# Gate and up projections with 512 moving columns behind one stationary operand

## The chip, the cores and the metric

The kernel runs on one core of a Trainium2 chip. The metric is device time in microseconds (us). The engines are named as the profile does: PE is TensorE (matmuls), PEld its weight loads, DVE is VectorE, ACT is ScalarE, POOL is GpSimd, and SP is the queue from which the DMAs are issued. A matmul has a stationary operand (lhsT, loaded first) and a moving operand, whose columns stream past it; the result is added up in a PSUM bank, which holds 512 fp32 columns for 128 partitions.

## The reference

Two layers of a trunk. Each makes modulation vectors, one input projection for two groups of heads (a gated delta rule and an attention), an output projection, a layer norm, and a SwiGLU feed-forward part with a second layer norm. 128 context tokens and 128 latent tokens go through the same weights, each group with its own modulation. The part that is changed is the feed-forward part:

```python
D_MODEL = 2048
D_FF = ((8 * D_MODEL + 767) // 768) * 256      # 5632
...
    h = x * (1.0 + sc2) + sh2
    gate, up = jnp.split(h @ w_gate_up, 2, axis=-1)
    ffn = (jax.nn.silu(gate) * up) @ w_down
    x = layer_norm(DN_ALPHA * x + g2 * ffn, ln2_g, ln2_b)
```

All is fp32.

## The kernel before

**Numbers in two halves.** The matmuls run in the type fp32r. To come near fp32, each operand is split: H is the value rounded to fp32r, L the rest. A product is then three passes: activation H by weight H, activation L by weight H, activation H by weight L. `wtile` brings two pairs of weight blocks with one DMA of 1 MB (tile `r`) and splits each pair: ACT copies to H (L391), DVE subtracts to L (L392). H and L have three buffers each, the DMA tiles four, which they share with the modulation weights (`rt`, `ra`).

**Gate and up.** The 5632 columns of gate and of up are cut into 22 chunks of 256 + 256 columns. A chunk runs over the 2048 rows of the weight, 16 blocks of 128, in four tiles `g` of four blocks. `col_mm` does one tile: for each half j of the tile (two blocks) and each of four groups b of 128 output columns (two of gate, two of up) the weight is stationary, and the 256 tokens are the moving columns. Lines L422 (H by H), L423 (activation L by weight H) and L426 (activation H by weight L) issue four, by blocks, and two matmuls. Two groups share a bank: `acc[0]` holds gate, `acc[1]` up. They come from the pool psA, which has three banks.

At the end of a chunk ACT takes the tanh of gate (L1234, tile `fth`), DVE makes silu (L1235) and the product with up (L1237, `hx`), and ACT (L1240) and DVE (L1241) split that into H and L of the hidden activations (`dH`, `dL`).

**Down.** After 16, 16 and 12 blocks of hidden columns the down projection runs over what is there (`HALVES`), in four column blocks of 512, with the hidden activations stationary and 512 weight columns moving (`row_mm`, L399, L400, L402). The result is added to `y`.

**Beside it.** In the feed-forward part of layer 0 DVE also computes modulation vectors of the next layer as dot products (`ada_dot`, L242, tile `rt`; a step is one DMA tile and two instructions, 16 steps a vector; four vectors in layer 0, one in layer 1). `fill` issues steps at a rate: `RATES[l][2]` is 0.55 in layer 0 and 0.15 in layer 1, and a quarter of it is added at each call, of which a chunk has 16. The order of instructions on each engine is set by the scheduler of the framework at build time; each engine then works in that order.

**Before and after.** The activations `h2` of the gate and up matmuls are built from the normed `y` by transposes into PSUM (L475), a modulation (L480 on DVE, L482 on ACT) and the split (L485, L486). The transposes use banks of the pool psG, whose tag `gu` has three. The same SBUF places hold, in turn, `h`, `mix` and `h2`, in four tiles hH0, hL0, hH1, hL1 of eight blocks each. The last column block of the down projection is kept for the `tail`, which runs the two token groups one after the other, so that the norm of one runs beside the matmuls of the other.

Of the kernel before, what the change touches and what calls it, by code (L numbers as in the profile page):

```python
# [106 lines left out]
def trunk(ctx: ExitStack, tc: tile.TileContext, A: dict, O: dict):  # L107
# [303 lines left out]
    def col_mm(acc, W, act, kts, first, last, hook=None):  # L411
        for j, (H, L) in enumerate(W):
# [3 lines left out]
            for b in range(4):  # L416
# [10 lines left out]
                if hook is not None and b % 2 == 1:  # L427
                    hook()

    def acc2():  # L430
        return [psA.tile([128, 512], F32, tag="acc", name="acc") for _ in range(2)]

    class Act:


        def __init__(self, tiles, per):
            self.t, self.per = tiles, per

# [4 lines left out]
        def stat(self, part, kt, s):  # L443
            return self.span(part, kt, 1)[:, 0, s, :]

        def mov(self, part, kt):
            return self.span(part, kt, 1)[:, 0].rearrange("p s t -> p (s t)")

    def new_act(name):
        return Act([tuple(htp.tile([128, 8, 2, 128], F32R, tag=f"h{x}{i}", name=f"{name}{x}{i}") for x in "HL")  # L450
                    for i in range(2)], 8)

# [157 lines left out]
    def mixer(l, h_act, P, first_layer, ax, xsrc, prev):  # L610

        W = A["p_in"][l]
        if True:
# [253 lines left out]
            def scratch(name, wide=False):  # L867

                if not first_layer:
                    return slab(name)[:, 0:1024 if wide else 512]  # L870
                if not scr:
                    scr["n"] = htp.tile([128, 2048], F32, tag="hH0", name="scr0")
                    scr["w"] = htp.tile([128, 2048], F32, tag="hL0", name="scr1")
# [323 lines left out]
    for l in range(NL):  # L1197
# [7 lines left out]
        with ExitStack() as fx:  # L1205
# [17 lines left out]
            for part, nkt in enumerate(HALVES):  # L1223
                hid = Act([(hidp.tile([128, 16, 2, 128], F32R, tag="dH", name="dH"),
                            hidp.tile([128, 16, 2, 128], F32R, tag="dL", name="dL"))], 16)
                for c in range(nkt // 2):
                    acc = acc2()
                    for g in range(4):
                        wt = wtile(A["p_gu"][l, hb // 2 + c, 2 * g:2 * g + 2], 4, 512)
                        col_mm(acc, wt, h2, range(4 * g, 4 * g + 4), g == 0, g == 3, lambda: fill(RATES[l][2] / 4))  # L1230
                    if part == 0 and c < 4:
                        norm.row(c)
                    th = tp.tile([128, 512], F32, tag="th", name="fth")
                    nc.scalar.activation(th, acc[0], AF.Tanh, scale=0.5)  # L1234
                    nc.vector.scalar_tensor_tensor(th, th, 1.0, acc[0], ALU.add, ALU.mult)  # L1235
                    hx = tp.tile([128, 512], F32, tag="hx", name="hx")
                    nc.vector.tensor_tensor(hx, th, acc[1], ALU.mult)  # L1237
                    H = hid.span(0, 2 * c, 2).rearrange("p k s t -> p (k s t)")
# [90 lines left out]
```

## Time and profile before

| | |
|---|---|
| median of 3 runs | 2731.94 us (2726.57 to 2733.45) |
| the profiled execution | 2723.28 us |
| its span, first to last instruction | 2721.5 us |
| PE busy | 2634.3 us, 97% |
| weight loads (PEld) busy | 2319.6 us, 85% |
| DVE busy | 2018.3 us, 74% |
| ACT busy | 1259.9 us, 46% |
| DMA | 659.08 MB, mean 242 GB/s |

The profile is of one execution, and its own time stands beside its span because durations come from it. Busy shares are means over stages that differ. A busy PE is not PE at its peak, because matmuls are pipelined: what one costs is read from the distance between two starts, not from its duration. The same holds for DVE, where an instruction starts a little before the one ahead of it has ended.

### The profile page before, as it was taken

How to read it: one execution, taken by the hardware profiler on the slowest of the kernel's cores; microseconds unless marked ns; L12 is line 12 of the kernel's file. 1: busy time of each engine (PE TensorE's matmuls, PEld its weight loads, DVE VectorE, ACT ScalarE, POOL GpSimd, SP SyncE). 2: the span in 40 equal slices, each digit the busy share in tenths (PEclk: the TensorE clock that was granted, in tenths of full speed). 3: DMA queues.
4: the chain of work that ended last, by engine and by line, in shares of the span. 5: the costliest groups of instructions: out<-in, count | busy, mean ns of one | idle time of the engine just before them, and what ended most of it. 6: DMA issues, size and time to landing. Idle time of an engine off the chain costs nothing.

```text
span 2721.5 us, 47282 instructions
## 1 busy us (share of the span) xinstructions
PE 2634.3 (97%) x19159; PEld 2319.6 (85%) x19159; DVE 2018.3 (74%) x2839; ACT 1259.9 (46%) x2150; POOL 74.9 (3%) x215
## 2 busy tenths in 40 slices
PE   7999999998999999999999999999899999999998
PEld 5888776677998899889988898767699989998996
DVE  3775888859988888999775768685866556665657
ACT  4333567634444444434454656663444444443442
POOL 0000101000000000000000101000000000000000
PEclk9999999998999999999999999999899999999999
DMA  7888765587888877887658544549566565666665
GB/s 288 305 321 303 265 234 175 184 311 248 297 282 297 307 288 269 294 309 285 236 206 284 191 164 157 175 171 311 192 227 218 204 227 209 213 218 209 234 213 162
DMA packets 170956, 659.08 MB, mean 242 GB/s; under 512 B 14592, under 2 KB 26098, under 8 KB 145522
## 3 DMA queue, kind: packets, MB, share of 16 engines
q1 hardware_dynamic: 170738, 656.07, 69.0%
q8 instruction: 150, 2.46, 0.4%
q14 instruction: 68, 0.56, 0.1%
HBM read 644.94 MB, written 11.08 MB: 241 GB/s over the span
## 4 chain that ended last, share of the span: by engine, by line
PE 71%; DVE 4%; DMA 2%; ACT 2%; issue 1%; POOL 1%; SPq 0%; DVEq 0%; POOLq 0%; ACTq 0%
PE acc L422 13%; PE acc L423 13%; PE acc L426 13%; PE acc L399 9%; PE acc L400 9%; PE acc L402 8%; PE psv L268 1%; DVE L L392 1%; DMA rt<-p_at 1%; PE pr L835 1%; ACT H L391 1%; PE pz L807 0%; PE pd L816 0%; PE pd L815 0%; DMA xp<-xm 0%
## 5 line engine op out<-in xcount | busy, mean ns | idle before, releaser
L391 ACT ACTIVATE H<-r 128x1024 fp32r<-128x1024 f32 (+1 forms) x770 | 801.6, 1043 | 1099.7 <-PE acc L423 589.1
L392 DVE TENSOR_TENSOR L<-r,H 128x1024 fp32r<-128x1024 f32 (+1 forms) x770 | 920.7, 1202 | 456.7 <-ACT H L391 447.1
L422 PE MATMUL acc<-h2H,H 128*128 128x256 f32 x2816 | 740.6, 285 | 9.4 <-DVE h2H L485 5.6
L423 PE MATMUL acc<-h2L,H 128*128 128x256 f32 x2816 | 739.2, 284 | 0.2
L426 PE MATMUL acc<-h2H,L 128*128 128x256 f32 x2816 | 567.7, 284 | 0.5 <-DVE L L392 0.5
L422 PEld LDWEIGHTS acc<-h2H,H 128*128 128x128 f32 x2816 | 541.1, 192 | 12.9 <-DVE h2H L485 6.4
L423 PEld LDWEIGHTS acc<-h2L,H 128*128 128x128 f32 x2816 | 541.4, 192 | 1.0 <-DVE h2L L486 0.8
L426 PEld LDWEIGHTS acc<-h2H,L 128*128 128x128 f32 x2816 | 439.7, 192 | 0.7 <-DVE L L392 0.7
L242 DVE SCALAR_TENSOR_TENSOR junk<-rt,cb 128x2048 f32<-128x2048 f32 x160 | 365.9, 2287 | 16.7 <-DMA rt<-p_at 16.5
L399 PE MATMUL acc<-H,dH 128*128 128x512 f32 x672 | 263.2, 392 | 1.3 <-DVE fth L1235 1.3
L400 PE MATMUL acc<-H,dL 128*128 128x512 f32 x672 | 262.3, 390 | 0.0
L422 PE MATMUL acc<-hH,H 128*128 128x256 f32 x768 | 208.4, 293 | 3.6 <-ACT H L391 3.6
L402 PE MATMUL acc<-L,dH 128*128 128x512 f32 x672 | 209.1, 392 | 0.9 <-DVE L L392 0.9
L423 PE MATMUL acc<-hL,H 128*128 128x256 f32 x768 | 203.4, 286 | 0.0
L422 PEld LDWEIGHTS acc<-hH,H 128*128 128x128 f32 x768 | 147.3, 192 | 16.8 <-issue 7.2
L399 PE MATMUL acc<-H,hH 128*128 128x392 f32 (+1 forms) x384 | 152.8, 398 | 7.6 <-ACT H L391 6.7
L426 PE MATMUL acc<-hH,L 128*128 128x256 f32 x768 | 157.3, 287 | 1.1 <-DVE L L392 0.8
L402 PEld LDWEIGHTS acc<-L,dH 128*128 128x128 f32 x672 | 126.1, 188 | 28.9 <-DVE L L392 1.3
L399 PEld LDWEIGHTS acc<-H,dH 128*128 128x128 f32 x672 | 126.3, 188 | 28.3 <-DVE fth L1235 1.7
L400 PEld LDWEIGHTS acc<-H,dL 128*128 128x128 f32 x672 | 126.2, 188 | 28.0
L423 PEld LDWEIGHTS acc<-hL,H 128*128 128x128 f32 x768 | 147.6, 192 | 0.1
L400 PE MATMUL acc<-H,hL 128*128 128x392 f32 (+1 forms) x384 | 143.2, 373 | 0.5 <-DVE hL L486 0.5
(289 smaller groups left out, 3317.1 us busy)
## 6 DMA issues: line engine op xcount, KB each, us to landing
r<-p_gu SPq DMA_DIRECT2D x176, 1024.0 KB
r<-p_dn SPq DMA_DIRECT2D x88, 1024.0 KB
ra<-p_av SPq DMA_DIRECT2D x80, 1024.0 KB
rt<-p_at SPq DMA_DIRECT2D x80, 1024.0 KB
r<-p_in SPq DMA_DIRECT2D x48, 1024.0 KB
ra<-p_a SPq DMA_DIRECT2D x32, 1024.0 KB
r<-p_o SPq DMA_DIRECT2D x32, 1024.0 KB
r<-p_in SPq DMA_DIRECT2D x24, 784.0 KB
```

The source lines that it names most:

```text
L242: nc.vector.scalar_tensor_tensor(side["junk"], r, 0.5, side["cb"][:, v, :], ALU.mult, ALU.mult, accum_out=sums[:, m, v:v + 1])
L268: nc.tensor.matmul(ps[32 * q:32 * q + 32, h * 256:(h + 1) * 256], lhsT=scT[:, 2 * kp + j, :], rhs=r[:, j, q * 256:(q + 1) * 256], start=h ...
L391: nc.scalar.activation(H[:, :w], rs_, AF.Copy)
L392: nc.vector.tensor_tensor(L[:, :w], rs_, H[:, :w], ALU.subtract)
L399: nc.tensor.matmul(a[:, :n], lhsT=act.stat(0, kt, s), rhs=H[:, i, :], start=(first and i == 0), stop=False)
L400: nc.tensor.matmul(a[:, :n], lhsT=act.stat(1, kt, s), rhs=H[:, i, :], start=False, stop=False)
L402: nc.tensor.matmul(a[:, :n], lhsT=act.stat(0, kt, s), rhs=L[:, i, :], start=False, stop=(last and i == 1))
L422: nc.tensor.matmul(a, lhsT=H[:, i, cs], rhs=xH, start=(f and i == 0 and b % 2 == 0), stop=False)
L423: nc.tensor.matmul(a, lhsT=H[:, i, cs], rhs=xL, start=False, stop=False)
L426: nc.tensor.matmul(a, lhsT=L[:, i, cs], rhs=xH, start=False, stop=(la and i == 1 and b % 2 == 1))
L835: nc.tensor.matmul(p[:, d * 128:(d + 1) * 128], lhsT=X[:, d, 0], rhs=v[:, d], start=True, stop=True)
```

## The change

The switch `WIDE` turns on a new way for the gate and up matmuls, in both layers. For each weight block and column group, activations H and L are the moving columns of one matmul of 512 behind the H weights; the matmul with the L weights adds 256 columns to the first half of the same bank. So each of the four column groups has a bank of its own, two from psA and two from `gu` of psG. At the end of a chunk ACT copies the second half of each bank to SBUF and DVE adds the first half, for gate into a new tile `gs`, for up into `hx`; tanh and the products then read SBUF. To make one moving operand of H and L they now lie in one tile, 8 KB per partition apart, which is why the four activation tiles become two. The rate of the dots in layer 0 goes from 0.55 to 0.5.

```diff
+WIDE = (True, True)
...
-RATES = ((2.2, 1.0, 0.55), (0.5, 0.6, 0.15))
+RATES = ((2.2, 1.0, 0.5), (0.5, 0.6, 0.15))
...
+    def wide_mm(accs, W, act, kts, first, last, hook=None):
+
+        for j, (H, L) in enumerate(W):
+            kk = kts[2 * j:2 * j + 2]
+            f = first and j == 0
+            la = last and j == len(W) - 1
+            for b in range(4):
+                a = accs[b]
+                cs = slice(b * 128, (b + 1) * 128)
+                for i, kt in enumerate(kk):
+                    nc.tensor.matmul(a.rearrange("p (a n) -> p a n", a=2), lhsT=H[:, i, cs], rhs=act.both(kt),
+                                     start=(f and i == 0), stop=False)
+                for i, kt in enumerate(kk):
+                    nc.tensor.matmul(a[:, 0:256], lhsT=L[:, i, cs], rhs=act.mov(0, kt), start=False, stop=(la and i == 1))
+                if hook is not None and b % 2 == 1:
+                    hook()
...
+        def both(self, kt):
+            i, k = divmod(kt, self.per)
+            return self.whole[i][:, :, k].rearrange("p a s t -> p a (s t)")
...
     def new_act(name):
-        return Act([tuple(htp.tile([128, 8, 2, 128], F32R, tag=f"h{x}{i}", name=f"{name}{x}{i}") for x in "HL")
-                    for i in range(2)], 8)
+        return Act([htp.tile([128, 2, 8, 2, 128], F32R, tag=f"h{i}", name=f"{name}{i}") for i in range(2)], 8)
...
-                    acc = acc2()
+                    if WIDE[l]:
+                        acc = [(psA, psG)[b % 2].tile([128, 512], F32, tag=("acc", "gu")[b % 2], bufs=3, name="acc") for b in range(4)]
+                    else:
+                        acc = acc2()
                     for g in range(4):
                         wt = wtile(A["p_gu"][l, hb // 2 + c, 2 * g:2 * g + 2], 4, 512)
-                        col_mm(acc, wt, h2, range(4 * g, 4 * g + 4), g == 0, g == 3, lambda: fill(RATES[l][2] / 4))
+                        (wide_mm if WIDE[l] else col_mm)(acc, wt, h2, range(4 * g, 4 * g + 4), g == 0, g == 3, lambda: fill(RATES[l][2] / 4))
...
+                    if WIDE[l]:
+                        gs = tp.tile([128, 512], F32, tag="gs", name="gs")
+                        for b in range(4):
+                            dst = (gs, hx)[b // 2][:, b % 2 * 256:b % 2 * 256 + 256]
+                            nc.scalar.activation(dst, acc[b][:, 256:512], AF.Copy)
+                            nc.vector.tensor_tensor(dst, acc[b][:, 0:256], dst, ALU.add)
+                        gate, up = gs, hx
+                    else:
+                        gate, up = acc
+                    nc.scalar.activation(th, gate, AF.Tanh, scale=0.5)
+                    nc.vector.scalar_tensor_tensor(th, th, 1.0, gate, ALU.add, ALU.mult)
+                    nc.vector.tensor_tensor(hx, th, up, ALU.mult)
```

In the changed kernel the lines from `wide_mm` on are some 20 to 33 higher: the wide matmul is L441, the one with the L weights L444, the copy L1263, the add L1264, tanh L1268, the products L1269 and L1270, the split L1273 and L1274. The lines of `wtile` and of the dots are one higher, L392, L393 and L243. The hidden activations and `h`, `mix`, `h2` keep their lines' order; only their tiles are joined.

The order on PE within one chunk of layer 0, first before the change. The names are the bank, the activations (h2H1 and h2L1, the second eight blocks) and the weight half; these are the matmuls of two blocks for one column group, and the first of the next.

```order
L422 MATMUL acc_9104<-h2H1_7446,H_9290 128x256
L423 MATMUL acc_9104<-h2L1_7447,H_9290 128x256
L422 MATMUL acc_9104<-h2H1_7446,H_9290 128x256
L423 MATMUL acc_9104<-h2L1_7447,H_9290 128x256
L426 MATMUL acc_9104<-h2H1_7446,L_9291 128x256 x2
L422 MATMUL acc_9104<-h2H1_7446,H_9290 128x256
```

The same place in the changed kernel, where h21 holds both halves:

```order
L441 MATMUL acc_9965<-h21_7440,H_10101 128x512 x2
L444 MATMUL acc_9965<-h21_7440,L_10102 128x256 x2
L441 MATMUL acc_9966<-h21_7440,H_10101 128x512 x2
L444 MATMUL acc_9966<-h21_7440,L_10102 128x256 x2
L441 MATMUL acc_9967<-h21_7440,H_10101 128x512 x2
```

Six matmuls for two blocks and a column group have become four, and each group names a bank of its own.

The order on DVE around the end of a chunk in layer 0, before: the subtractions L for the next weights, the dots, and the operations of the evacuation.

```order
L392 TENSOR_TENSOR L_9113<-r_9106,H_9112 128x1024
L242 SCALAR_TENSOR_TENSOR junk_7559,dot_7685<-rt_9198,cb_7556 128x2048
L392 TENSOR_TENSOR L_9167<-r_9164,H_9166 128x1024
L1235 SCALAR_TENSOR_TENSOR fth_9097<-fth_9097,acc_8851 128x512
L242 SCALAR_TENSOR_TENSOR junk_7559,dot_7685<-rt_9198,cb_7556 128x2048
L1237 TENSOR_TENSOR hx_9100<-fth_9097,acc_8852 128x512
L392 TENSOR_TENSOR L_9171<-r_9164,H_9170 128x1024
```

The same place in the changed kernel:

```order
L243 SCALAR_TENSOR_TENSOR junk_7552,dot_9243<-rt_10141,cb_7549 128x2048
L393 TENSOR_TENSOR L_10168<-r_10165,H_10167 128x1024
L393 TENSOR_TENSOR L_10172<-r_10165,H_10171 128x1024
L1264 TENSOR_TENSOR gs_10147<-acc_9965,gs_10147 128x256
L1264 TENSOR_TENSOR gs_10147<-acc_9966,gs_10147 128x256
L1264 TENSOR_TENSOR hx_10146<-acc_9967,hx_10146 128x256
L243 SCALAR_TENSOR_TENSOR junk_7552,dot_9243<-rt_10249,cb_7549 128x2048
L393 TENSOR_TENSOR L_10210<-r_10207,H_10209 128x1024
L393 TENSOR_TENSOR L_10214<-r_10207,H_10213 128x1024
L1264 TENSOR_TENSOR hx_10146<-acc_9968,hx_10146 128x256
L1269 SCALAR_TENSOR_TENSOR fth_10145<-fth_10145,gs_10147 128x512
```

The adds of the first three banks stand behind two subtractions for the next chunk and ahead of a dot; the fourth stands behind that dot and two more subtractions.

The order on DVE near the end of layer 0, in the second column block of the last part of the down projection (y is the block's sum, e0 and e1 are places for weights of the last block), in the changed kernel:

```order
L613 BN_STATS stats_7557<-y_6907 128x6
L611 TENSOR_TENSOR y_6907<-y_6907,gr_13238 128x512
L243 SCALAR_TENSOR_TENSOR junk_7552,dot_12023<-rt_13446,cb_7549 128x2048
L393 TENSOR_TENSOR L_13460<-r_13457,H_13459 128x1024
L393 TENSOR_TENSOR e0_13510<-r_13511,e0_13510 128x1024
L393 TENSOR_TENSOR L_13464<-r_13457,H_13463 128x1024
```

Before, the last dot stood ahead of the end of the last chunk but one of gate and up, and here were only subtractions and the residual.

## Rows read from the trace of the kernel before

**Rows 1.** The page: busy us, share and instructions by engine; the chain.

```profile
PE 2634.3 (97%) x19159; PEld 2319.6 (85%) x19159; DVE 2018.3 (74%) x2839; ACT 1259.9 (46%) x2150; POOL 74.9 (3%) x215
...
PE acc L422 13%; PE acc L423 13%; PE acc L426 13%; PE acc L399 9%; PE acc L400 9%; PE acc L402 8%; PE psv L268 1%; DVE L L392 1%; DMA rt<-p_at 1%; PE pr L835 1%; ACT H L391 1%; PE pz L807 0%; PE pd L816 0%; PE pd L815 0%; DMA xp<-xm 0%
```

**Rows 2.** Stretch: PE, PEld, DVE, ACT, POOL busy us (instructions), clock, DMA.

```profile
648.00:653.00 5.00, 4.88 (x23) 4.69 (x23) 4.78 (x9) 1.62 (x5) 0.00 (x0) 0.50 0.35 146
970.25:1110.06 139.81, 138.88 (x1154) 138.39 (x1153) 125.18 (x122) 57.85 (x60) 0.00 (x0) 1.00 0.78 278
2200.30:2222.28 21.98, 21.98 (x97) 18.03 (x96) 14.06 (x12) 9.57 (x11) 0.00 (x0) 1.00 0.65 239
2252.33:2413.80 161.47, 161.47 (x1346) 161.32 (x1345) 99.85 (x96) 67.49 (x70) 0.00 (x0) 1.00 0.60 212
1337.00:1387.00 50.00, 50.00 (x226) 41.29 (x225) 37.37 (x41) 24.03 (x24) 0.00 (x0) 1.00 0.67 232
```

**Rows 3.** PE in time, gate/up, layer 1 (start, us, operation); 32 matmuls left out.

```profile
2249.97 0.28 PE L422 MATMUL acc<-h2H,H 128*128 128x256 f32 x1
...
2253.93 0.28 PE L423 MATMUL acc<-h2L,H 128*128 128x256 f32 x1
```

**Rows 4.** ACT in time, layer 1: the tanh of a chunk; six left out.

```profile
2252.33 0.60 ACT L1234 ACTIVATE fth<-acc 128x512 f32<-128x512 f32 x1 [0.62 <-PE acc L426]
...
2413.80 0.60 ACT L1234 ACTIVATE fth<-acc 128x512 f32<-128x512 f32 x1 [0.62 <-PE acc L426]
```

**Rows 5.** PE's waits, 650 to 1340, then 1965 to 2650: us, times, longest.

```profile
PE acc L399 <- DVE fth L1235: 1.3, 1, 1.3
PE acc L422 <- DVE fth L1235: 0.8, 1, 0.8
...
PE acc L422 <- DVE fth L1235: 2.9, 2, 1.9
```

**Rows 6.** PE in time, down projection, layer 1; 95 matmuls left out.

```profile
2200.32 0.39 PE L399 MATMUL acc<-H,dH 128*128 128x512 f32 x1
...
2222.29 0.39 PE L399 MATMUL acc<-H,dH 128*128 128x512 f32 x1
```

**Rows 7.** The page, gate/up matmul groups: count, busy us, mean ns, idle before.

```profile
L422 PE MATMUL acc<-h2H,H 128*128 128x256 f32 x2816 | 740.6, 285 | 9.4 <-DVE h2H L485 5.6
...
L426 PE MATMUL acc<-h2H,L 128*128 128x256 f32 x2816 | 567.7, 284 | 0.5 <-DVE L L392 0.5
```

**Rows 8.** Evacuations of the input projection: count, ns min/median/max, first and last start.

```profile
L659 DVE TENSOR_TENSOR pad<-acc,pad x120: 412/418/428, 74.3 to 315.8; 128x256 f32<-128x256 f32 x120
...
L661 ACT ACTIVATE pad<-acc x48: 362/384/413, 34.4 to 1628.2; 128x256 f32<-128x256 f32 x48
```

**Rows 9.** DVE in time, gate/up, layer 0.

```profile
993.64 1.22 DVE L392 TENSOR_TENSOR L<-r,H 128x1024 fp32r<-128x1024 f32 x1
994.78 0.68 DVE L1235 SCALAR_TENSOR_TENSOR fth<-fth,acc 128x512 f32<-128x512 f32 x1
995.37 2.29 DVE L242 SCALAR_TENSOR_TENSOR junk<-rt,cb 128x2048 f32<-128x2048 f32 x1
...
997.58 2.36 DVE L392 TENSOR_TENSOR L<-r,H 128x1024 fp32r<-128x1024 f32 x2
```

**Rows 10.** PE, then DVE in time, start of the gate/up stage of layer 0.

```profile
647.40 0.80 PE L422 MATMUL acc<-h2H,H 128*128 128x256 f32 x2 [4.40 <-DVE h2H L485]
648.32 0.58 PE L423 MATMUL acc<-h2L,H 128*128 128x256 f32 x1
...
647.58 0.68 DVE L486 TENSOR_TENSOR h2L<-hf,h2H 128x512 fp32r<-128x512 f32 x1
...
650.14 0.40 DVE L480 TENSOR_SCALAR hf<-pt,G,B 128x128 f32<-128x128 f32 x1
```

**Rows 11.** DVE groups, gate/up, layer 0: count, busy us, mean ns, idle before.

```profile
L242 DVE SCALAR_TENSOR_TENSOR junk<-rt,cb 128x2048 f32<-128x2048 f32 x27 | 61.7, 2286 | 2.7 <-DMA rt<-p_at 2.7
L392 DVE TENSOR_TENSOR L<-r,H 128x1024 fp32r<-128x1024 f32 x48 | 58.1, 1221 | 11.0 <-ACT H L391 10.9
```

More of the change, by code (lines that the diff above doesn't have):

```diff
@@ L436, in __init__ @@
         def __init__(self, tiles, per):
-            self.t, self.per = tiles, per
+            self.whole = tiles
+            self.t, self.per = [(t[:, 0], t[:, 1]) for t in tiles], per
         def span(self, part, kt, n):
@@ L871, in scratch @@
                 if not scr:
-                    scr["n"] = htp.tile([128, 2048], F32, tag="hH0", name="scr0")
-                    scr["w"] = htp.tile([128, 2048], F32, tag="hL0", name="scr1")
+                    both = htp.tile([128, 4096], F32, tag="h0", name="scr")
+                    scr["n"], scr["w"] = both[:, 0:2048], both[:, 2048:4096]
                     scr["ni"] = 0
@@ L1223, in trunk @@
             for part, nkt in enumerate(HALVES):
-                hid = Act([(hidp.tile([128, 16, 2, 128], F32R, tag="dH", name="dH"),
-                            hidp.tile([128, 16, 2, 128], F32R, tag="dL", name="dL"))], 16)
+                hid = Act([hidp.tile([128, 2, 16, 2, 128], F32R, tag="d", name="d")], 16)
                 for c in range(nkt // 2):
-                    acc = acc2()
+                    if WIDE[l]:
+                        acc = [(psA, psG)[b % 2].tile([128, 512], F32, tag=("acc", "gu")[b % 2], bufs=3, name="acc") for b in range(4)]
+                    else:
+                        acc = acc2()
                     for g in range(4):
                         wt = wtile(A["p_gu"][l, hb // 2 + c, 2 * g:2 * g + 2], 4, 512)
-                        col_mm(acc, wt, h2, range(4 * g, 4 * g + 4), g == 0, g == 3, lambda: fill(RATES[l][2] / 4))
+                        (wide_mm if WIDE[l] else col_mm)(acc, wt, h2, range(4 * g, 4 * g + 4), g == 0, g == 3, lambda: fill(RATES[l][2] / 4))
                     if part == 0 and c < 4:
@@ L1233, in trunk @@
                     th = tp.tile([128, 512], F32, tag="th", name="fth")
-                    nc.scalar.activation(th, acc[0], AF.Tanh, scale=0.5)
-                    nc.vector.scalar_tensor_tensor(th, th, 1.0, acc[0], ALU.add, ALU.mult)
                     hx = tp.tile([128, 512], F32, tag="hx", name="hx")
-                    nc.vector.tensor_tensor(hx, th, acc[1], ALU.mult)
+                    if WIDE[l]:
[10 more added lines that the diff above has]
+                    nc.vector.tensor_tensor(hx, th, up, ALU.mult)
                     H = hid.span(0, 2 * c, 2).rearrange("p k s t -> p (k s t)")
@@ L1289, in trunk @@
                 if i < 2:
-                    HL = [htp.tile([128, 8, 2, 128], F32R, tag=f"h{x}{i}", name=f"e{x}{i}").rearrange("p a b c -> p (a b c)")
-                          for x in "HL"]
+                    HL = htp.tile([128, 2, 2048], F32R, tag=f"h{i}", name=f"e{i}")
+                    HL = [HL[:, 0], HL[:, 1]]
                     store = [(HL[0][:, j * 1024:(j + 1) * 1024], HL[1][:, j * 1024:(j + 1) * 1024]) for j in range(2)]
```

## The prediction

> **What bounds the kernel now.** The page comes first [rows 1]. TensorE (PE) is busy for 97% of the span, VectorE (DVE) for 74%, and the three matmul lines of the gate/up stage, L422, L423 and L426, alone hold 39% of the chain that ended last. A busy PE is not yet a bound one, so the second view is the table by stretches [rows 2]: in layer 0's gate/up stage PE is busy for 138.88 of 139.81 us and issues 1154 matmuls, in layer 1's for all of 161.47 us with 1346. The spacing of starts says what one costs: 33 steps in 3.96 us, 120.0 ns each [rows 3]. A chunk has 16 x 4 x 3 = 192 of them, 23.04 us; eight of the tanh that ends a chunk stand 161.47 us apart for seven chunks, 23.07 each [rows 4]. Of a stage of 22 chunks almost nothing is waiting: PE waited for the vector work at chunk ends for 1.3 + 0.8 us in layer 0 and 2.9 us in layer 1 [rows 5]. So the gate/up stage is set by how fast PE gets through its passes, in both layers. DVE is the second: in layer 0 it is busy for 125.18 of those 139.81 us (90%), in layer 1 for 99.85 of 161.47 (62%) [rows 2].
>
> **The passes.** Per contraction block and 128 output columns there were three passes of 256 columns, each with its own weight load; now there is one of 512 and one of 256, with the same columns in all. What a removed pass is worth follows from two spacings: 256 columns take 120.0 ns [rows 3], and in the down projection 96 passes of 512 columns lie in 21.97 us, 228.8 ns each [rows 6]. So a column costs (228.8 - 120.0) / 256 = 0.425 ns, and a pass 11.2 ns beside its columns. Two passes of 256 are 240.0 ns, one of 512 is 228.8. There are 2816 such pairs, the count of L422 [rows 7] (22 chunks x 2 layers x 16 blocks x 4 column groups): 2816 x 11.2 ns = **31.5 us** less. A chunk falls from 23.04 to 64 x (228.8 + 120.0) ns = 22.32 us.
>
> What the trace of before does not show is a moving operand of 512 columns that lies in two runs of 256, 8 KB apart; the down projection's 512 are one run. From below it costs nothing; from above as much as the second start that was removed, 11.2 ns, which takes all 31.5 us away. I take nothing, since the 256-column passes stream at the same rate per column as the single run.
>
> The Trainium skill ("TensorE: Matmul & The Clock Gate", section "Wait — 56ns, not 53.3ns?") puts the fixed cost of a warm matmul beside its columns at about 2.5 ns. By that the removed passes would give 2816 x 2.5 ns = 7 us, an estimate from that page. The rows have a weight load before every matmul, and measure 11.2 ns, so the sum goes by the rows.
>
> **The evacuation.** Each chunk gains four copies of 256 columns on ScalarE (ACT) and four adds of 256 on DVE. The nearest rows, the PSUM evacuations of the input projection, have 384 ns for such a copy and 418 ns for such an add [rows 8]. DVE starts its next instruction a little before the last one ends: 0.59 us from start to start for a 512-column operation that shows 0.68, 1.14 for the split's subtraction L392, 2.21 for half a modulation dot L242 [rows 9]; an add of 418 ns therefore takes about 0.33. ACT goes from 57.85 / 6 = 9.6 to 11.2 us a chunk [rows 2]: covered. DVE in layer 0, per chunk: eight L392 9.12, three evacuation operations 1.77, and the dots, of which the fill rate now brings 16 x 0.5 / 4 = 2.0 steps instead of 2.2, two halves each: 8.84 instead of 9.72. With the adds, 1.32, that is 21.05 us, where before it was 20.6. PE's chunk is 22.32, so the adds are hidden with 1.27 us to spare; uncovered they cost 44 x 1.32 = 58 us. In layer 1 the spare is over 6 us a chunk.
>
> Does PE wait for a bank? A chunk's first bank is full 3 x 0.70 = 2.1 us before the chunk ends (0.70 us is two blocks of one column group, 2 x 0.349) and comes back to PE as the next chunk's third bank, 1.4 us after the end: 3.5 us for a copy and an add. Before, a bank had 1.44 + 1.44 = 2.9 us for a 0.60 us tanh and a 0.68 us DVE operation. In the order of DVE the first three adds now stand ahead of the next dot. So the 5.0 us of PE's waits for the chunk end [rows 5] do not grow; I count no gain, and at the lower end of the range 4 us.
>
> DMA is left out of the sum: a chunk has four weight tiles and 2.0 instead of 2.2 dot tiles of 1 MB, in a time that is 3% shorter, the same 278 GB/s [rows 2].
>
> **Start of each gate/up stage.** PE ran the H half of the first block at 647.40 and waited for the L half until 648.32, after the DVE subtraction that began at 647.58 [rows 10]. The wide pass needs both halves at once, so two short passes no longer run ahead: 2 x 0.22 us at the clock of this stretch, 0.50 of full speed, 1.2 GHz, where 23 matmuls filled 5.00 us [rows 2]. Two of the four banks are also ones that the transposes just before have used. A DVE instruction that reads such a bank begins as late as 650.14 [rows 10]; at 6 x 0.22 = 1.3 us a group PE reaches the fourth bank 3.9 us after 648.3. From below 0, from above 2 us; I take 1 us, twice: **+2 us**.
>
> **End of layer 0.** The slower rate spreads the 64 dot steps to the end of the layer; in the order of DVE one now stands in the second of the last column blocks of the down projection and one in the first, where before there were none. There DVE is busy for 37.37 of 50 us [rows 2]; two steps add 8.84, so they fit with 3.8 us left. Queued behind them are subtractions for the next weights and the residual that frees a bank, for which PE waits. From below 0, from above all 8.84 us; I take **+2 us**, nearer to the lower end because the idle exceeds them.
>
> The sum: -31.5 + 2 + 2 = **-27.5 us**. The profiled execution took 2723.28 us, its span 2721.5; the median of the timed runs is 2731.94, 8.7 above it. I carry the difference over to the median: **2704 us**.
>
> **Rivals.** First, DVE becomes layer 0's bound. For: beside its work it waited there for 14.63 / 6 = 2.44 us a chunk, 10.9 of those 14.63 us for ACT's H, which waits for PE to free a buffer, 2.7 for a dot tile [rows 2, 11]; only 1.27 may remain. Against: each wait for H is one that PE's own pace sets, and shrinks when DVE is late. If the chunk stays at its measured 139.81 / 6 = 23.3 us, layer 0 gives nothing of its 16: 2704 + 16 = 2720.
>
> Second, the two runs of the moving operand cost the second start after all: the change does not do what it says. No PE gain, 4 us of costs: 2736.
>
> Third, the pass that is left gets slower per column than the down projection's, so that a removed pass brings a quarter of the 11.2 ns: 8 us, less 4 us of costs, 2728. Against: 0.425 ns a column and 11.2 ns a pass fit the spacings of both stages. The 2.5 ns that the Trainium skill gives, above, would come out close to this.
>
> Fourth, on the other side: a dot stands in front of an add, and PE waits at the third bank of the next chunk in layer 0. Price: one half dot, 2.21 us x 22 = 49 us, 2753. It decides from 28 / 22 = 1.3 us a chunk. For: dots are 8.84 of DVE's 21.05 us. Against: the order of DVE, and 3.5 us of room.
>
> Fifth, the cycling through four banks opens small gaps, PE's clock falls from 2.4 to 1.2 GHz in part of the stage. Rows: at clock 0.50 the stretch 648 to 653 stood behind a PE idle of 4.40 us; in the stages the clock is 1.00 [rows 2, 10]. 768 columns at 0.22 us per 256 are 0.65 instead of 0.349 us, so a tenth of the stages' 44 x 22.32 = 982 us at the lower clock costs 85 us: 2789. The Trainium skill (same page, "A second HAM failure mode: psum-queue depth-cycling") reports such an oscillation for a kernel that cycled banks; in this trace the down projection alternates between two banks at clock 1.00, which does not bear it out.
>
> **Numbers.** Chances: forecast 0.70; DVE bound in layer 0 0.13; two runs 0.06; small fixed cost 0.03; bank wait 0.06; clock 0.02. The forecast's own range is 2694 (4 us of waits gone, and a fast set: the runs spread over 6.9 us) to 2714 (upper ends at both places). The range over all, 2693 to 2726, takes in the first rival and part of the second's costs (half a start per wide pass, 16 us); the second to fifth stay mostly outside, 0.17. A measurement of this kernel can tell about 0.3%, 8 us. Faster by more than that: forecast and first rival, 0.83; within: second and third, 0.09; slower: fourth and fifth, 0.08.
>
> **What would show it.** Two spacings in the changed gate/up stage, 229 ns after a 512-column matmul and 120 after a 256-column one; 128 matmuls and 22.3 us a chunk in both layers; DVE in layer 0 near 94% busy, with PE still without idle; waits of PE on the adds only at isolated places. I am wrong on the passes if the wide spacing is near 240 ns, on DVE if layer 1's chunks fall to 22.3 and layer 0's stay near 23.3, on the banks if the third matmul group of a chunk waits for an add, and on the end of layer 0 if PE idles by more than 2 us there among the last blocks.

## The result, and the profile after

The changed kernel takes 2684.91 us (median of 4 runs, 2683.92 to 2688.60), the kernel before in the same comparison 2729.26 us (4 runs, 2725.07 to 2733.45): a ratio of 0.9844, 95% interval 0.9830 to 0.9857. Between the profiled executions it is 2723.28 to 2683.92, 39.4 us less. The forecast was 2704, with 27.5 us less between executions: the sign is right, the gain was put too small, and the time lies below the range.

The page after, its busy line and the chain by line:

```profile
PE 2596.5 (97%) x16343; PEld 2157.9 (80%) x16343; DVE 2071.7 (77%) x3015; ACT 1315.4 (49%) x2326; POOL 74.0 (3%) x215
...
PE acc L441 23%; PE acc L444 12%; PE acc L400 9%; PE acc L401 9%; PE acc L403 9%; PE psv L269 1%; PE acc L423 1%; PE acc L424 1%; PE acc L427 1%; DVE L L393 1%; PE pr L857 1%; PE pz L829 1%; ACT H L392 0%; PE pd L838 0%; DMA gr<-grow 0%
```

Against [rows 1] PE has 2816 matmuls fewer. It is still busy for 97%, and the two gate/up lines L441 and L444 hold 35% of the chain where the three before had 39; DVE has gone from 74 to 77%. The stretches show by how much each stage is nearer to its second limit (columns as in [rows 2]): five chunks of layer 0, 50 us at the end of layer 0, and the second part of layer 1.

```profile
720.68:832.15 111.47, 111.47 (x642) 97.25 (x641) 108.40 (x121) 54.22 (x72) 0.00 (x0) 1.00 0.80 291
1318.00:1368.00 50.00, 50.00 (x221) 40.60 (x220) 49.03 (x54) 22.85 (x25) 0.00 (x0) 1.00 0.78 276
2203.60:2381.90 178.30, 178.30 (x1025) 155.57 (x1024) 122.09 (x135) 86.26 (x111) 0.00 (x0) 1.00 0.62 217
```

In layer 0 PE has no idle at all in five chunks, although DVE is busy for 108.40 of 111.47 us (97%). At the end of layer 0 DVE is busy for 49.03 of 50 us where it was 37.37, and PE still for all 50. The granted clock is 1.00 of its 2.4 GHz in each. The tanh of a chunk, ACT in time, layer 0, four left out:

```profile
720.68 0.62 ACT L1268 ACTIVATE fth<-gs 128x512 f32<-128x512 f32 x1
...
832.15 0.62 ACT L1268 ACTIVATE fth<-gs 128x512 f32<-128x512 f32 x1
```

Five chunks in 111.47 us are 22.29 us each, in the layer where DVE was feared as the bound; layer 1 has 178.30 / 8 = 22.29 as well, where [rows 4] had 23.07. PE in time, in layer 1:

```profile
2068.28 0.63 PE L441 MATMUL acc<-h,H 128*128 128x512 f32 x2
2068.74 0.40 PE L444 MATMUL acc<-h,L 128*128 128x256 f32 x2
...
2071.76 0.63 PE L441 MATMUL acc<-h,H 128*128 128x512 f32 x2
```

From 2068.28 to 2071.76 lie ten pairs: 348 ns each. With 120.0 ns for the pass that was left as it was [rows 3], the wide pass takes 228, the same as one run of 512 columns in the down projection [rows 6]. So the two runs of 256 columns, 8 KB apart, cost nothing that the pair shows. Only the pair is firm: in the second part of layer 1 the single starts stand 233 ns apart behind a wide pass and 115 behind a narrow one, not 229 and 120 as the prediction gave for its signs, and no run tells why the pair is split so.

PE's waits, 650 to 1400, then 1940 to 2680 (us, times, longest):

```profile
PE acc L441 <- DVE h L508: 3.5, 1, 3.5
PE acc L400 <- DVE h L507: 0.5, 1, 0.5
...
PE acc L444 <- DVE L L393: 0.6, 1, 0.6
```

The waits for `fth` of [rows 5] are gone, and no wait for an add has come in their place. The first line is the start of layer 0's stage, the second that of layer 1's input projection. The DVE groups of the five chunks answer to [rows 11]:

```profile
L393 DVE TENSOR_TENSOR L<-r,H 128x1024 fp32r<-128x1024 f32 x40 | 48.8, 1221 | 3.1 <-ACT H L392 2.6
L243 DVE SCALAR_TENSOR_TENSOR junk<-rt,cb 128x2048 f32<-128x2048 f32 x21 | 47.9, 2282 | 0.0
```

DVE now waits for ACT's H for 2.6 us in five chunks, where it was 10.9 in six, and for no dot tile.

**Where the 39.5 us of the span went.** PE's start times of the first matmul of each part, taken from PE in time, cut both spans into the same parts:

| part (us) | before | after | difference |
|---|---|---|---|
| up to the gate/up stage of layer 0 | 647.40 | 650.00 | +2.6 |
| gate/up, layer 0, 22 chunks | 513.6 | 493.2 | -20.4 |
| first two down parts, layer 0 | 177.3 | 175.9 | -1.4 |
| last down part of layer 0 to gate/up of layer 1 | 613.9 | 616.5 | +2.6 |
| gate/up, layer 1, 22 chunks | 514.8 | 493.3 | -21.5 |
| first two down parts, layer 1 | 175.8 | 175.8 | 0.0 |
| last down part to the end | 78.7 | 77.4 | -1.3 |

The 44 chunks give 41.9 us. At 23.04 - 22.29 = 0.75 us a chunk the passes explain 33.0 of it. The other 9 is what the experiments are about.

### The profile page after: what moved, and what is told of

It is laid out like the page before. It is cut to its first block, busy times and chain, and to the rows that moved or that the text cites. A ratio compares the mean times of both kernels' runs of the same rounds, so it can differ in the third digit from the quotient of the medians.

```text
span 2682.0 us, 42000 instructions
## 1 busy us (share of the span) xinstructions
PE 2596.5 (97%) x16343; PEld 2157.9 (80%) x16343; DVE 2071.7 (77%) x3015; ACT 1315.4 (49%) x2326; POOL 74.0 (3%) x215
## 4 chain that ended last, share of the span: by engine, by line
PE 72%; DVE 3%; ACT 2%; DMA 2%; issue 1%; POOL 1%; SPq 0%; DVEq 0%; POOLq 0%; ACTq 0%
PE acc L441 23%; PE acc L444 12%; PE acc L400 9%; PE acc L401 9%; PE acc L403 9%; PE psv L269 1%; PE acc L423 1%; PE acc L424 1%; PE acc L427 1%; DVE L L393 1%; PE pr L857 1%; PE pz L829 1%; ACT H L392 0%; PE pd L838 0%; DMA gr<-grow 0%
## 5 line engine op out<-in xcount | busy, mean ns | idle before, releaser
L392 ACT ACTIVATE H<-r 128x1024 fp32r<-128x1024 f32 (+1 forms) x770 | 801.5, 1043 | 1005.8 <-PE acc L441 467.5
L393 DVE TENSOR_TENSOR L<-r,H 128x1024 fp32r<-128x1024 f32 (+1 forms) x770 | 920.9, 1201 | 386.7 <-ACT H L392 374.2
L441 PE MATMUL acc<-h,H 128*128 128x512 f32 x2816 | 887.4, 397 | 5.6 <-DVE h L508 5.6
L444 PEld LDWEIGHTS acc<-h,L 128*128 128x128 f32 x2816 | 530.3, 188 | 126.7 <-DVE L L393 1.5
L444 PE MATMUL acc<-h,L 128*128 128x256 f32 x2816 | 554.6, 278 | 0.6 <-DVE L L393 0.6
L441 PEld LDWEIGHTS acc<-h,H 128*128 128x128 f32 x2816 | 430.8, 189 | 7.2 <-DVE h L508 6.4
L243 DVE SCALAR_TENSOR_TENSOR junk<-rt,cb 128x2048 f32<-128x2048 f32 x160 | 365.3, 2283 | 1.6 <-DMA rt<-p_at 1.6
L400 PE MATMUL acc<-H,d 128*128 128x512 f32 x672 | 263.1, 392 | 0.0
L401 PE MATMUL acc<-H,d 128*128 128x512 f32 x672 | 263.0, 392 | 0.0
L423 PE MATMUL acc<-h,H 128*128 128x256 f32 x768 | 208.7, 293 | 4.1 <-ACT H L392 4.1
L403 PE MATMUL acc<-L,d 128*128 128x512 f32 x672 | 208.2, 391 | 0.0
L424 PE MATMUL acc<-h,H 128*128 128x256 f32 x768 | 203.5, 286 | 0.0
L400 PE MATMUL acc<-H,h 128*128 128x392 f32 (+1 forms) x384 | 152.9, 399 | 9.3 <-ACT H L392 8.7
L423 PEld LDWEIGHTS acc<-h,H 128*128 128x128 f32 x768 | 147.7, 192 | 16.7 <-issue 7.8
L427 PE MATMUL acc<-h,L 128*128 128x256 f32 x768 | 157.0, 286 | 3.0 <-DVE L L393 2.6
L403 PEld LDWEIGHTS acc<-L,d 128*128 128x128 f32 x672 | 126.1, 188 | 28.3 <-DVE L L393 0.4
L400 PEld LDWEIGHTS acc<-H,d 128*128 128x128 f32 x672 | 126.2, 188 | 27.7 <-DVE gr L607 0.5
L401 PEld LDWEIGHTS acc<-H,d 128*128 128x128 f32 x672 | 126.2, 188 | 27.3 <-DVE d L1274 0.3
L424 PEld LDWEIGHTS acc<-h,H 128*128 128x128 f32 x768 | 147.9, 193 | 0.1
L401 PE MATMUL acc<-H,h 128*128 128x392 f32 (+1 forms) x384 | 143.5, 374 | 0.0
L427 PEld LDWEIGHTS acc<-h,L 128*128 128x128 f32 x768 | 120.2, 193 | 5.4 <-DVE L L393 4.4
```

The source lines that it names most:

```text
L243: nc.vector.scalar_tensor_tensor(side["junk"], r, 0.5, side["cb"][:, v, :], ALU.mult, ALU.mult, accum_out=sums[:, m, v:v + 1])
L392: nc.scalar.activation(H[:, :w], rs_, AF.Copy)
L393: nc.vector.tensor_tensor(L[:, :w], rs_, H[:, :w], ALU.subtract)
L400: nc.tensor.matmul(a[:, :n], lhsT=act.stat(0, kt, s), rhs=H[:, i, :], start=(first and i == 0), stop=False)
L401: nc.tensor.matmul(a[:, :n], lhsT=act.stat(1, kt, s), rhs=H[:, i, :], start=False, stop=False)
L403: nc.tensor.matmul(a[:, :n], lhsT=act.stat(0, kt, s), rhs=L[:, i, :], start=False, stop=(last and i == 1))
```

## The experiments

Theory A: the passes give 33.0 us, and the four banks most of the rest, because PE no longer waits for a bank at chunk ends. Rival B: the banks and the new evacuation bring the gain, not the passes. Rival C: the slower dot rate, with another order on DVE, took the waits away. Rival D: DVE is about to become layer 0's bound.

**The wide pass cut in two** (`e1_split`), on the changed kernel:

```diff
-nc.tensor.matmul(a.rearrange("p (a n) -> p a n", a=2), lhsT=H[:, i, cs], rhs=act.both(kt), ...)
+nc.tensor.matmul(a[:, 0:256], lhsT=H[:, i, cs], rhs=act.mov(0, kt), ...)
+nc.tensor.matmul(a[:, 256:512], lhsT=H[:, i, cs], rhs=act.mov(1, kt), ...)
```

> Theory A: the matmul passes alone account for 33.0 of the change's 39.4 us between the profiled executions (44 chunks, 23.04 to 22.29 us), and the four banks for most of the rest, because PE no longer waits at chunk ends. With each 512-column matmul cut into two of 256 behind the same weights, and banks, copies and adds as in the changed kernel, a chunk should take 192 x 120.0 ns = 23.04 us again with no wait of PE for DVE at a chunk's end: 2685 + 33 = 2718 us. Rival B: banks and evacuation bring the gain, the passes little: chunks below 22.6 us and 2685 to 2695. Rival C: the waits left because of the slower dot rate and the order of DVE; that gives 2718 here too, and is told apart by the next two kernels.

2722.51 us (11 runs; 0.9977 of before, 0.9969 to 0.9986). PE in time, layer 1, 31 matmuls left out, and then PE's waits in the two stretches:

```profile
2329.81 0.28 PE L442 MATMUL acc<-h,H 128*128 128x256 f32 x1
...
2333.66 0.29 PE L442 MATMUL acc<-h,H 128*128 128x256 f32 x1
```

```profile
PE acc L441 <- DVE y L1308: 1.0, 1, 1.0
...
PE acc L441 <- DVE gs L1264: 1.3, 1, 1.3
```

32 steps in 3.85 us are 120.3 ns: the passes alone bring the chunk back to 23.04 us. Its 44 chunks take 1022.4 us, 35.9 more than in the changed kernel; 2.3 of that are the waits of L441 for `y` and `gs`, which the changed kernel doesn't have. That leaves 33.6 for the passes. Rival B falls. The time is 4.5 us above what A gave: the waits, and stretches that weren't edited and came out longer, such as the input projection of layer 1 (414.0 us against 412.4).

**The old matmuls with the new tiles and rate** (`e2_old_mm`), on the changed kernel:

```diff
-WIDE = (True, True)
+WIDE = (False, False)
```

> The old matmuls, two banks and old evacuation, with the joined activation tiles and the dot rate 0.5. Theory A (banks): the waits of PE for the first product of a chunk's evacuation stay, 5 to 6 us in all, and the time stays within 3 us of the kernel before, 2729. Rival C (rate and DVE order): the waits fall to 1 us or less, 2721 to 2723.

2728.59 us (11 runs; 0.9999 of before, 0.9989 to 1.0009). PE's waits in the two stretches:

```profile
PE acc L423 <- DVE fth L1269: 1.3, 1, 1.3
...
PE acc L423 <- DVE fth L1269: 3.5, 2, 1.9
```

The waits for `fth` are as in [rows 5], 4.8 us here. Rate and tiles together leave the time where it was; rival C falls.

**The old matmuls with a bank pool each for gate and up** (`e3_six_banks`), on the kernel of `e2_old_mm`:

```diff
-RATES = ((2.2, 1.0, 0.5), (0.5, 0.6, 0.15))
+RATES = ((2.2, 1.0, 0.55), (0.5, 0.6, 0.15))
...
-acc = acc2()
+acc = [p.tile([128, 512], F32, tag=t, bufs=3, name="acc") for p, t in ((psA, "acc"), (psG, "gu"))]
```

> The old matmuls and old evacuation with the old rate 0.55, but the gate bank from one pool of three and the up bank from the other, so that a bank has more than a chunk of time before it is needed again. Theory A: waits at the chunk ends and the small gaps at the reuse of a bank go, about 8 us: 2729 - 8 = 2721, chunks at 23.04 us throughout. Rival C: the waits stay, 2727 to 2731.

2718.04 us (7 runs; 0.997 of before, 0.9959 to 0.9981, which is 5 to 11 us). All of PE's waits in the two stretches that fall on a gate/up line:

```profile
PE acc L423 <- DVE h L507: 4.4, 1, 4.4
PE acc L424 <- DVE h L508: 0.3, 1, 0.3
...
PE acc L423 <- DVE h L507: 1.2, 1, 1.2
PE acc L424 <- DVE h L508: 0.3, 1, 0.3
```

What is left are the starts of the two stages. The 44 chunks take 1021.4 us, 7.0 less than before, and the first two down parts of layer 0 176.0, 1.3 less. So the room of the banks alone is worth 8.3 us in a kernel that has all its passes, of which the rows of waits had shown 5.0. A wait of L426 for weights in layer 1, 0.5 us in the view before, is gone too. Most of the rest are gaps of 0.1 to 0.3 us at the reuse of a bank, such as one from 1067.49 to 1068.03 between matmuls two steps apart, which no view of waits lists: a matmul's modelled duration is 285 ns at a spacing of 120 [rows 3, 7], so that 0.165 us of a gap is covered by it.

**Fewer free banks in the changed kernel** (`e6_tight`):

```diff
-(psA, psG)[b % 2] ... ("acc", "gu")[b % 2]
+(psA, psG)[b // 3] ... ("acc", "gu")[b // 3]
```

> The changed kernel with three of a chunk's four banks from the pool of three and the fourth from the other, so that the bank filled first in a chunk is wanted again at once by the next chunk's first group instead of 1.4 us after. Theory A (room of the banks is worth what the passes don't explain): PE waits for copy and add at most chunk ends, 0.5 to 2 us each in layer 0 and 0 to 0.5 in layer 1, 8 to 30 us in all, about 2700. Rival (banks have nothing to do with it): within 3 us of the changed kernel, 2682 to 2688.

2690.72 us (4 runs; 0.9868 of before, 0.9851 to 0.9885), 5.8 above the changed kernel and between the two theories. PE's waits for the adds in layer 1:

```profile
PE acc L441 <- DVE gs L1264: 0.9, 2, 0.7
```

In layer 0 the view lists none. The 2.1 us that a full bank still has are almost always enough for a copy and an add, so my 0.5 to 2 us a chunk were far too much. Of the 5.8 us 4.0 lie in the two gate/up stages and 1.7 in the first two down parts of layer 0; where no wait is listed, their cause is not shown. A bank of the old kernel had 2.9 us and PE waited 5.0 in all, here it has 2.1 and PE waits 0.9. That suggests that the old kernel was hurt by what a bank waited for, tanh and a DVE operation behind the dots, as much as by the number of banks; no run parts the two.

**The dot rate of layer 0**, on the changed kernel at 0.55 (`e4_rate`), 0.6 (`e10_rate60`) and 0.65 (`e7_rate65`):

```diff
-RATES = ((2.2, 1.0, 0.5), (0.5, 0.6, 0.15))
+RATES = ((2.2, 1.0, 0.55), (0.5, 0.6, 0.15))
```

> The changed kernel with the dot rate back at 0.55. By the prediction's count DVE then has 21.9 of 22.3 us of work a chunk in layer 0. Theory A: four banks give room, so within 3 us of the changed kernel, 2682 to 2688. Rival C: waits of PE at chunk ends of layer 0 return, 3 to 8 us more, 2688 to 2693. Rival D (DVE as the bound of layer 0 with so little to spare): layer 0's chunks lengthen to over 22.6 us, 7 us more or beyond.

> The changed kernel with a dot rate of 0.6 in layer 0: 2.4 steps a chunk, so by the prediction's count DVE has 2.4 x 4.42 + 9.12 + 1.77 + 1.32 = 22.8 us of work in a PE chunk of 22.3. At 0.55 (21.9 us) the time didn't move, at 0.65 (23.7) it rose by 30 us. Theory A (the count is right): 0.5 us a chunk for some 20 chunks, 6 to 12 us, 2691 to 2697. Rival (a threshold further up, waits only beyond 23 us): within 4 us of the changed kernel.

> The changed kernel with a dot rate of 0.65 in layer 0: 2.6 instead of 2.0 steps a chunk, so by the prediction's count DVE has 2.6 x 4.42 + 9.12 + 1.77 + 1.32 = 23.7 us of work in a PE chunk of 22.3. Theory A (the count is right, and DVE becomes the bound from there): layer 0's chunks 23.7 us until the steps run out after some 19 chunks, 20 to 27 us more, about 2708. Rival (the count is too high by over 6%, DVE still keeps up): chunks of 22.3 us, within 4 us of the changed kernel.

2685.27 us at 0.55 (0.9847 of before, 0.9833 to 0.9860), 2697.72 at 0.6 (0.9888, 0.9861 to 0.9915), 2715.49 at 0.65 (0.9956, 0.9941 to 0.9970): 0.4, 12.8 and 30.6 us above the changed kernel. PE's waits from 650 to 1400 at 0.6, and at 0.65, there with a stretch of layer 0's second part:

```profile
PE acc L441 <- DVE gs L1264: 2.9, 3, 1.4
PE acc L400 <- DVE gs L1264: 1.9, 1, 1.9
```

```profile
PE acc L444 <- DVE L L393: 6.7, 11, 1.6
PE acc L441 <- DVE gs L1264: 4.1, 4, 1.9
```

```profile
850.00:1110.00 260.00, 255.45 (x1335) 215.76 (x1334) 258.31 (x265) 117.99 (x143) 0.00 (x0) 1.00 0.82 304
```

At 0.65 DVE is busy for 258.31 of 260 us, and PE waits for subtractions and adds. The count of DVE's work gives the point at which the time rises: 21.9 us in a chunk of 22.3 costs nothing in all, 22.8 and 23.7 cost. At 0.55 the 22 chunks of layer 0 take 495.9 us, 2.7 more than in the changed kernel, and the last down part, in which no dots are left, 1.8 less. The size comes out above theory A both times, 12.8 for 6 to 12 and 30.6 for 20 to 27, and it isn't spread chunk by chunk. At 0.6 the chunks of layer 0 take 499.9 us, 6.7 more, and the first two down parts 185.3, 9.4 more; at 0.65 the first eight chunks alone take 18.6 more. Rival D is true as a limit, but begins 0.1 of a rate above where the change put it.

**Also in the input projection of layer 1** (`e8_win`): the column chunks there call `wide_mm`, with three banks from psA and one from `gu`.

```diff
-acc = acc2()
+acc = acc2() if not wide else [(psA, psG)[b // 3].tile([128, 512], F32, tag=("acc", "gu")[b // 3], bufs=3, name="acc") for b in range(4)]
```

> The changed kernel with the same way of matmuls also in the column chunks of the input projection of layer 1: 384 pairs of 256-column passes become 512-column ones, three banks from one pool and one from the other, 24 more adds on DVE. Theory A (a removed pass is worth 11.7 ns wherever PE sets the pace): 384 x 11.7 = 4.5 us less, 2680. Rival (here the banks are shared with the work of the heads, and the reuse of a bank waits for copy and add): no gain or up to 10 us more, 2685 to 2695.

2684.43 us (5 runs; 0.9841 of before, 0.9826 to 0.9857): no gain that can be told. Its input projection takes 410.1 us, in the changed kernel 412.4, but in `e4_rate`, where nothing of it was edited, 408.8. A few us from order alone hide what 384 passes could give; the question stays open.

**What a pass costs beside its columns** (`e5_cols`, `e9_cols2`, `e11_half_load`), on the changed kernel:

```diff
-nc.tensor.matmul(a.rearrange("p (a n) -> p a n", a=2), lhsT=H[:, i, cs], rhs=act.both(kt), ...)
+nc.tensor.matmul(a[:, 0:384].rearrange("p (a n) -> p a n", a=3), lhsT=H[:, i, cs], rhs=act.three(kt), ...)
...
-nc.tensor.matmul(a[:, 0:256], lhsT=L[:, i, cs], rhs=act.mov(0, kt), ...)
+nc.tensor.matmul(a[:, 0:128], lhsT=L[:, i, cs], rhs=act.mov(0, kt)[:, 0:128], ...)
```

`three` gives three blocks of 128 in one run; where it is used, the copy at the end of a chunk reads columns 128 to 384. `e5_cols` has both edits in both layers, `e9_cols2` the first in layer 1 and the second in layer 0, `e11_half_load` the second in both layers, with 64 stationary columns:

```diff
-nc.tensor.matmul(a[:, 0:256], lhsT=L[:, i, cs], rhs=act.mov(0, kt), ...)
+w = 128 if la else 64
+nc.tensor.matmul(a[0:w, 0:128], lhsT=L[:, i, b * 128:b * 128 + w], rhs=act.mov(0, kt)[:, 0:128], ...)
```

> What a pass costs beside its columns. In the gate/up matmuls the wide pass has 384 moving columns instead of 512 (a block of 128 of them is another's, so half of the product activation L by weight H is left out and part is wrong) and the pass with the L weights 128 instead of 256 (half of it left out). Theory A (a pass costs 11.7 ns plus 0.423 ns a column, the line through 120.0 ns at 256 columns and 228.3 at 512): 174.1 ns and 65.9 ns from start to start. Rival (the weight load ahead of each matmul sets a lower limit for a pass, so that the line doesn't hold below 256 columns): 174 ns for the wide pass, but clearly more than 66 for the narrow one. Layer 0 will then be bound by DVE, so the spacings are read in layer 1.

PE in time in layer 1, 384 and 128 columns:

```profile
2300.05 0.57 PE L441 MATMUL acc<-h,H 128*128 128x384 f32 x2
...
2318.39 0.57 PE L441 MATMUL acc<-h,H 128*128 128x384 f32 x2
```

The clock is 1.00 in this stretch and the three that follow. 32 groups of two wide and two narrow passes in 18.34 us are 573.1 ns each, not 480: the line through 256 and 512 does not hold below 256, or not at 384.

> The kernel with 384 and 128 columns took 573.1 ns for two passes of each, where the line through 256 and 512 columns gives 480. Now layer 0 has 512 columns in the wide pass and 128 in the one with the L weights (half of that product is left out), layer 1 has 384 and 256 (half of the product activation L by weight H is left out, part of it is another block's). Theory F (a pass of 128 columns doesn't get shorter than 112.4 ns, the limit set by the weight load behind it or ahead of it): 228.3 + 112.4 = 340.7 ns a pair in layer 0, 174.1 + 120.0 = 294.1 in layer 1. Rival G (the pass of 384 is what was long, 220.7 ns): 228.3 + 65.9 = 294.2 in layer 0 and 220.7 + 120.0 = 340.7 in layer 1.

PE in time, first 512 and 128 columns in layer 0, then 384 and 256 in layer 1:

```profile
968.07 0.68 PE L442 MATMUL acc<-h,H 128*128 128x512 f32 x2
968.59 0.33 PE L447 MATMUL acc<-h,L 128*128 128x128 f32 x2
968.76 0.68 PE L442 MATMUL acc<-h,H 128*128 128x512 f32 x2
...
974.25 0.68 PE L442 MATMUL acc<-h,H 128*128 128x512 f32 x2
...
2330.13 0.52 PE L442 MATMUL acc<-h,H 128*128 128x384 f32 x2
...
2344.37 0.52 PE L442 MATMUL acc<-h,H 128*128 128x384 f32 x2
```

Nine groups in 6.18 us are 343.3 ns a pair in layer 0; 24 in 14.24 us are 296.7 in layer 1. Theory F holds: 384 columns take 296.7 - 120.0 = 176.7 ns, and 128 take 343.3 - 228.3 = 115 (by the first kernel 573.1 / 2 - 176.7 = 110), twice the 128 x 0.423 = 54 ns of the columns alone.

> A pair of 512 and 128 columns took 343.3 ns in layer 0 of the last kernel, so the pass of 128 columns took 115 where its columns alone need 53. Here both layers have 512 and 128 columns, and the stationary operand of the pass with the L weights has 64 columns instead of 128 (in all tiles of a chunk but the last half one, so three quarters of that product are left out). In the order two wide, two narrow, the second narrow pass has the load of a full wide weight behind it, the first only that of half a weight. Theory W (the limit is the weight load that runs beside the pass): the first narrow pass falls to about 60 ns, the second stays at 115: 2 x 228.3 + 60 + 115 = 632 ns for four. Rival M (a matmul has that least distance whatever the load): 687 ns for four as before.

PE in time, 512 and 128 columns, the narrow pass with half a weight:

```profile
2478.10 0.68 PE L441 MATMUL acc<-h,H 128*128 128x512 f32 x2
2478.61 0.28 PE L445 MATMUL acc<-h,L 128*64 128x128 f32 x2
2478.73 0.68 PE L441 MATMUL acc<-h,H 128*128 128x512 f32 x2
...
2485.70 0.68 PE L441 MATMUL acc<-h,H 128*128 128x512 f32 x2
```

Twelve groups in 7.60 us are 633 ns, as theory W gave, where rival M gave 687. If a matmul with 64 stationary columns were itself the quicker one, both narrow passes would gain, and the group would take 2 x 228.3 + 2 x 60 = 577. So the least distance of two matmuls is set here by the load of the next weights, which runs beside the pass. Which pass of the group bears it the starts don't tell as the theory has it: the two narrow ones go from 0.17 us (968.59 to 968.76) to 0.12 (2478.61 to 2478.73), and the two wide ones take 0.51 to 0.52 us in both kernels, not 2 x 228.3 ns = 0.46. Only the sums of groups are firm. The Trainium skill ("TensorE: Matmul & The Clock Gate", section "LDWEIGHTS (loading the stationary operand)") has the load time grow with the stationary columns alone, an estimate of 107 ns for 128; the 110 to 115 measured agree with it, and so does the fall with 64 columns.

These three kernels have fewer columns to compute and yet took 2732.98, 2746.63 and 2826.47 us (one run each). The loss lies in layer 0, whose 22 chunks take 546, 613 and 608 us, where they take 493 in the changed kernel. What DVE and PE waited for in `e9_cols2` from 700 to 830, layer 0:

```profile
DVE junk L243 <- DMA rt<-p_at: 23.9, 8, 4.8
PE acc L447 <- DVE L L393: 16.0, 9, 3.4
```

DVE is not full there (102.7 of 130 us), but a dot whose tile has not come holds up the subtraction behind it, and PE waits for that. This is close to the fourth rival's mechanism, which had an add behind the dot. Why the tiles come late in these kernels no run shows.

## Why the prediction was too small

**The passes: right.** 11.2 ns a removed pass, 31.5 us, measured 33.0 (a pair takes 348.3 rather than 348.8 ns, by the ten pairs and the chunk), shown by `e1_split` as 33.6. The price was read where it just holds: 256 columns take 120.0 ns, and 128 columns still 110 to 115, so that passes cut shorter would have cost far more than the line says. The figure of the Trainium skill, 2.5 ns a pass ("TensorE: Matmul & The Clock Gate", "Wait — 56ns, not 53.3ns?"), gave an estimate of 7 us; the runs bear out the rows. What makes up the 11.7 ns at 384 and 512 columns, where the load has time to spare, no run tells.

**The step that failed:** "So the 5.0 us of PE's waits for the chunk end [rows 5] do not grow; I count no gain". The working just ahead of it had found more room for a bank and a shorter way to free it, and it was used only to exclude a loss. The banks alone give 8.3 us by `e3_six_banks`: the 5.0 that the rows showed, and 3.3 mostly in gaps that no row of waits lists. Even the low end, 4 us, was below it. A view that shows them was at hand: the step from one part's first matmul to the next's, against its count times 120.0 ns. Layer 0's second part took 186.0 us for 184.3 us of passes, with 0.8 us of waits listed; with the six banks it takes 184.3. The first part of a layer is no measure of it, since it begins at the lower clock: its excess, 4.1 us in layer 0, is still 3.4 with six banks.

**Starts, +2: paid, and won back by the clock.** The first wide pass did come later, as argued. From the last two matmuls of the output projection to the first of gate/up it is 17.88 us before and 18.67 after in layer 0, 13.68 and 15.17 in layer 1. PE in time, start of layer 0, and then the first 10 us of both stages, in the changed kernel and in `e3_six_banks` (columns as in [rows 2]):

```profile
650.00 1.22 PE L441 MATMUL acc<-h,H 128*128 128x512 f32 x2 [3.49 <-DVE h L508]
```

```profile
650.00:660.00 10.00, 10.00 (x44) 8.60 (x45) 9.30 (x15) 3.74 (x6) 0.00 (x0) 0.75 0.16 47
1935.54:1945.54 10.00, 10.00 (x49) 8.71 (x50) 8.26 (x15) 3.98 (x7) 0.00 (x0) 0.86 0.23 63
```

```profile
649.59:659.59 10.00, 9.66 (x57) 9.37 (x58) 9.01 (x15) 3.73 (x6) 0.00 (x0) 0.69 0.26 99
1949.65:1959.65 10.00, 9.66 (x56) 9.37 (x57) 7.55 (x15) 3.59 (x6) 0.00 (x0) 0.67 0.04 8
```

The 2.3 us come back in the first part, which runs 2.8 us over its passes in layer 0 and 1.8 in layer 1, where `e3_six_banks` has 3.4 and 3.6. The clock accounts for that: its mean over these 10 us is 0.75 and 0.86 instead of 0.69 and 0.67, 2.5 us more of full clock. The prediction had no term for it, and it is luck: in `e4_rate`, with the same matmuls and starts as late, the mean clock is 0.73 and 0.79, the first parts run 3.8 and 2.3 us over, and only 0.9 of the 2.3 come back.

**End of layer 0, +2: 1.8, as forecast.** The last down part takes 66.2 instead of 65.5 us from its first to its last two matmuls, and the input projection of layer 1 begins another 1.0 later: PE waits there for `h` (L507), which DVE makes behind the residual. From one first matmul to the other it is 70.5 instead of 68.8 us, and with the rate back at 0.55 (`e4_rate`) 68.8 again. DVE took the dots up into its idle, as the stretch of 50 us shows, but not without delay.

**The evacuation: hidden,** as costed. DVE in layer 0 was forecast at 94%, and is at 97% in five chunks that hold 21 half dots instead of 20.

**The carry-over.** "I carry the difference over to the median" added 8.7 us to the forecast. The profiled execution of before was simply a quick one: the runs of before in the four timed comparisons go from 2721.76 to 2734.17 us, with medians from 2727.11 to 2729.26. The changed kernel's median is 1.0 above its profiled execution.

Of the miss of 19 us, 8.3 are the banks, 7.7 the carry-over, 1.5 the passes, 2.1 the cost of the starts that the clock gave back, and 0.2 the end of layer 0. That is 19.8, which is as near as single executions allow: stretches that the working didn't touch moved by up to 2 us each way (the first 480 us took 2.0 longer after, the output projection of layer 1 2.0 less), and stay unexplained.

**The rivals.** DVE as the bound of layer 0, held at 0.13, is excluded at this rate by the 22.29 us of both layers, and shown to begin near 0.6. The two runs and the slower column are excluded by the 348 ns of a pair, the bank wait by the rows of waits, the clock by its 1.00.

## What to carry to other kernels

Price a removed pass from two spacings of the same trace, and know where the line ends: here a pass of 128 columns took 110 to 115 ns because of the load of the weights behind it, and one of 256 took 120.0. By that, joining two of 128 would give some 100 ns, an estimate that no run tried, where joining two of 256 gave 11.7. When a change gives a buffer more room, count the waits that it takes away as well as those it doesn't add, and measure them as the excess of a stage over its count of steps, since short gaps hide behind modelled durations. An engine that is off the path at 97% is still off it, but a few per cent more of work on it turns into time, here somewhat more than the count gave.

## What was not expected of the hardware

A wait of PE costs more than its length. `e9_cols2`, PE in time around a wait in layer 0, and the stretches (columns as in [rows 2], the clock third from the end):

```profile
759.79 0.68 PE L442 MATMUL acc<-h,H 128*128 128x512 f32 x2
763.68 0.44 PE L447 MATMUL acc<-h,L 128*128 128x128 f32 x2 [3.20 <-DVE L L393]
...
766.48 1.16 PE L442 MATMUL acc<-h,H 128*128 128x512 f32 x2
767.44 0.52 PE L447 MATMUL acc<-h,L 128*128 128x128 f32 x2
767.76 1.04 PE L442 MATMUL acc<-h,H 128*128 128x512 f32 x2
```

```profile
755.00:760.00 5.00, 5.00 (x31) 4.39 (x31) 2.15 (x1) 2.10 (x4) 0.00 (x0) 1.00 0.90 372
760.00:765.00 5.00, 1.60 (x8) 0.93 (x7) 4.97 (x7) 0.00 (x0) 0.00 (x0) 1.00 0.25 75
765.00:770.00 5.00, 4.85 (x18) 4.17 (x19) 3.92 (x8) 3.47 (x6) 0.00 (x0) 0.66 0.83 345
```

After a wait of 3.20 us the clock is 0.66 in the next stretch, full in the one ahead (the 0.00 of the middle row is neither of the two levels, and eight matmuls ran there); from 766.48 to 767.76 four passes take 1.28 us, where they take 0.687 at clock 1.00 (two pairs of 343.3 ns). In the three kernels with fewer columns, the mean clock in layer 0 is about 0.9, in `e11_half_load` from 700 to 830 us

```profile
700.00:830.00 130.00, 107.25 (x560) 81.93 (x559) 97.67 (x106) 48.67 (x65) 0.00 (x0) 0.86 0.60 226
```

0.86, with PE busy for 107 of 130 us. So these kernels, with less to do on PE, took longer than the one they came from: PE waited for the engine that feeds it, and ran part of the time behind such waits at the lower clock.
